# Tokens transposed without their norm, layer 3's norm factor applied at the banks, six context k-tiles first, and another ending, in a four-layer backbone on one core

## The chip, the cores and the metric

The kernel runs on one core of a Trainium2 chip. What counts is the device time of one execution in microseconds (us). The kernel before took 2101.03 us, the median of three timed runs (2100.48 to 2101.74). One further execution was recorded by the hardware profiler; it took 2097.56 us.

## The reference, cut to what matters

A latent stream of 256 tokens and a context stream of 256 tokens, both 2048 wide and in float32, pass through four layers: Fourier mixing, mLSTM, attention, and Fourier mixing again. Every layer normalises the tokens, scales and shifts them by factors made from a conditioning vector, mixes them, and adds the gated result to the residual. The last layer works on the latent stream alone, and a normalisation ends the whole.

```python
for i in range(DEPTH):
    shift, scale, gate = jnp.split(sc @ ada_w[i] + ada_b[i], 3, axis=-1)
    hx = _rmsnorm(x, norm_g[i]) * (1.0 + scale[:, None]) + shift[:, None]
    ...   # the same for the context, with its own shift, scale and gate
    y_x = branch(hx)      # Fourier: (fourier_mix(hx) * silu(hx @ w_gate)) @ w_out
    x = x + gate[:, None] * y_x
    ...
return _rmsnorm(x, final_g)
```

`_rmsnorm(x, g)` is `x * rsqrt(mean(x*x) + eps) * g`. The factor rsqrt(...), called rstd below, is one number for each token. "Stream 0" in the kernel is the context (columns 0 to 255 of a k-tile), "stream 1" the latent (columns 256 to 511).

## The kernel before

**Layout.** Activations lie transposed: 16 k-tiles, each 128 features by 512 token columns. A product in full precision is made of three matmuls in a faster 32-bit format: every operand is split into a high part (`h`, `wh`) and a low part (`l`, `wl`), and h·wh, h·wl and l·wh are summed in a PSUM bank (line 309). Weights stream in as 512 KB tiles for two k-tiles each (`make_w`, line 264); ScalarE makes `wh` (267), VectorE `wl` (268). Three such pairs are held (`WHL`).

**gemm (line 274).** In orientation A the weights are stationary and four banks of 128 output features by the token columns are filled; in orientation B the tokens are stationary and each bank holds 128 tokens by 512 output features. Eight weight tiles are walked through. For the last `tail` of them the loop goes bank by bank, so that one bank ends after the other and its `done` reads it while the next one is filled. With `begin`, used at the head of layers 1 and 2, the first four k-tiles are done for stream 0 alone, then for stream 1; `begin(kt)` is called after each k-tile of stream 0, and `Norm.begin` (429) uses it at k-tiles 0 and 2 for the two halves of stream 1's rstd: the column sums and their root (`rstd_cols`, 376), then the row that holds rstd for each token, spread over all partitions (`rstd_rows`, 392). `modulate` (401) makes h and l of one k-tile from the residual, the row, and the layer's factor and shift.

**Order.** Only TensorE's order is written out by hand; the instructions of the other engines are ordered by the framework's scheduler under their dependences. DMA starts lie on SyncE's queue, those of the last output partly on ScalarE's. Background work (`bg`, the conditioning products of later layers on VectorE, line 228) and filler work on TensorE (`fill`, `mixes`) are drawn from queues at hand-set rates, some steps for each piece of a gemm.

**Layer 0's start (lines 586 to 730).** The conditioning vector is spread over all partitions (`cb`, eight calls of `spread`, 239: VectorE builds diagonals, TensorE transposes them, VectorE copies the bank out). Four 1 MB tiles of tokens land; their squares are summed; r0 (rstd as a column) is made. `begin(k2, ...)` then runs for k2 = 0 to 7. It makes the scale and the shift of two k-tiles from eight 512 KB tiles of the conditioning weights (`ada_pe`, 189: the matmuls of line 198, four landings for the scale, then four for the shift), with pieces of layer 0's first gemm or of the Fourier mixing between them. For k2 = 0 the pieces are `turn(j)` (636): the tokens are multiplied by r0 (640, 642), transposed (646), and copied to `xT` (648). `modulated(k2)` (651) applies scale and shift on ScalarE (657) and splits into h and l (372, 373). The landing places are six buffers of their own and four of the `araw` pool; from k2 = 3 they are the four and up to three unused pairs of `l` tiles (`land_l`, 180).

**Layer 2's end and layer 3's head (lines 1270 to 1310).** `out_proj` (445) adds the gated product to the residual bank by bank (467) and sums squares (473, 474). Layer 3's scale and shift are finished. Then come the transposes of the residual to token-major `xtk` (1287, 1288), rstd as column and row, and `modulate` for each k-tile ahead of the gate product `gated(0)` (its `done` is line 1304).

**The ending (lines 1357 to 1394).** For every group of 512 output features and both banks of 128 tokens, `done` forms t = bank·gate and t = x + t (1376, 1377), sums its squares (1378), and apart from that makes t2 = bank·(gate·final_g) (1385) and x = x·final_g + t2 (1386, 1387). In the last group the sum gives rstd (1381, 1382, 1389), which multiplies the 2048 columns on VectorE (1152 of them, 1391) and ScalarE (896, 1392), and two DMAs carry them out.

Of the kernel before, what the change touches and what calls it, by code (L numbers as in the profile page):

```python
# [28 lines left out]
BR1O, BR2 = 0.5, 0.25  # L29
# [20 lines left out]
def _build(tc, nc, top, A, out):  # L50
# [23 lines left out]
    adab = cp.tile([P, 4, 3, 2, KT], F32, name="adab")  # L74
# [89 lines left out]
    def ada_finish(l, s, kts, src, nv):  # L164

        v0 = 2 - nv
        dst = ada[:, l, s, v0:2, kts]
        V.tensor_tensor(dst, src, adab[:, l, s, v0:2, kts], ALU.add)
        if s == SC:
            V.tensor_tensor(dst, dst, ng[:, l, v0:2, kts], ALU.mult)  # L170
# [9 lines left out]
    def land_l(kt):  # L180

        def get(src):
            raws = [hlp.tile([P, 512], F32, tag=f"l{k}", name=f"lraw{k}") for k in (kt, kt + 1)]
            for i in range(2):
                Q.dma_start(raws[i], src[:, i, :])
            return raws
        return get
# [51 lines left out]
    def spread(dst, col):  # L239

        d = ap_.tile([P, 2, 512], F32, tag="araw", name="adiag", bufs=ARAW)[:, 0, :]
# [34 lines left out]
    def gemm(hl, orient, t0, t1, done, first=False, used=None, halves=False, begin=None, tail=2):  # L276
# [46 lines left out]
        for k2 in range(2 if begin else 0, 8 - tail):  # L323
# [39 lines left out]

    def hl_pair(kt):
        h = hlp.tile([P, 512], F32R, tag=f"h{kt}", name=f"h{kt}")
        l = hlp.tile([P, 512], F32R, tag=f"l{kt}", name=f"l{kt}")
        return h, l
# [24 lines left out]
    def rstd_rows(pp, r, nt):  # L392

        ps = bank()
        for i in range(nt):
            d = pp.tile([P, 256], F32, tag="mu", name="rdiag", bufs=2)[:, :128]
            V.tensor_scalar(d, ones, r[:, i:i + 1], None, ALU.mult)
# [14 lines left out]
    class Norm:  # L412
# [16 lines left out]
        def begin(self, kt):  # L429
            if kt in (0, 2):  # L430
# [14 lines left out]
    def out_proj(pp, px, l, hl, old, new_dram, c0, rates, tag="xf", bufs=5, gate=None, norm=None, t0=None):  # L445
# [6 lines left out]
        for g in range(4):  # L452
# [5 lines left out]
            def done(b, ps, stream=None):  # L458
# [6 lines left out]
                for s in streams:  # L465
                    a = 256 * s - c0
                    V.scalar_tensor_tensor(rn[:, b, a:a + 256], ps[:, 256 * s - o:256 * s - o + 256],  # L467
                                           ada[:, l, GA, s, kt:kt + 1], ro[:, b, a:a + 256], ALU.mult, ALU.add)
                if kt == 0:
# [115 lines left out]
    with ExitStack() as st:  # L585
# [7 lines left out]
        for v in range(2):  # L593
            for j in range(4):
                o = cb[:, v, 512 * j:512 * j + 512]
                drain(spread(lambda ps, o=o: V.tensor_copy(o, ps), cvec[:, v, 4 * j:4 * j + 4]))
        ss = p0.tile([P, 4, 4], F32, name="ss")
        xt = []
        for j in range(4):
# [3 lines left out]
            for i in range(4):  # L603
# [3 lines left out]
                else:  # L607
                    junk = ap_.tile([P, 1024], F32, tag="junk", name="ajunk", bufs=1)[:, :512]
                    V.scalar_tensor_tensor(junk, x[:, i, :], 1.0, x[:, i, :], ALU.mult, ALU.mult,
                                           accum_out=ss[:, i, j:j + 1])  # L610
            if j == 2:

                S.activation(dummy, ss[:, 1, 2:3], AF.Sqrt)
            if j == 0:
                Q.dma_start(adab, A["adab"])
                Q.dma_start(ng, A["ng"])
        for l in range(4):

            V.tensor_scalar(adab[:, l, SC], adab[:, l, SC], 1.0, None, ALU.add)
# [3 lines left out]
        V.reciprocal(r0, r0)  # L623

# [9 lines left out]
        xT = []  # L634

        def turn(j):

            for t in range(4):
                if t % 2:
                    S.activation(xt[j][:, t, :], xt[j][:, t, :], AF.Copy, scale=r0[:, t:t + 1])  # L640
                else:
                    V.tensor_scalar(xt[j][:, t, :], xt[j][:, t, :], r0[:, t:t + 1], None, ALU.mult)
            for i in range(4):
                ps = bank()
                for t in range(4):
                    T.transpose(ps[:, 128 * t:128 * t + 128], xt[j][:, t, 128 * i:128 * i + 128], ident)
                x = hlp.tile([P, 512], F32, tag=f"h{4 * j + i}", name=f"xT{4 * j + i}")
                (S.copy if i % 2 else V.tensor_copy)(x, ps)
                xT.append(x)

        def modulated(k2):

            for kt in (2 * k2, 2 * k2 + 1):
                u = p0.tile([P, 512], F32, tag="mu2", name="u", bufs=2)
                for s in range(2):
                    c = slice(256 * s, 256 * s + 256)
                    S.activation(u[:, c], xT[kt][:, c], AF.Identity, scale=ada[:, 0, SC, s, kt:kt + 1],
                                 bias=ada[:, 0, SH, s, kt:kt + 1])
                hl[kt] = split_into(kt, u)

        araws, mixes = land(ap_, "araw", ARAW), Weave()

        def begin(k2, places):


            make_w()
            place = [places]
            for n, _ in enumerate(chain(*(ada_pe(0, s, k2, cpad, place) for s in (SC, SH)))):
                if k2 == 0:
                    if n % 2:  # L670
                        turn(n // 2)
                elif n in (1, 2, 5, 6):
                    next(first)
                else:
                    mixes.give(MIX0)
            modulated(k2)
# [9 lines left out]
        with ExitStack() as st2:  # L686
            pf = pool(st2, "l0f", reuse_waits="tile")

            def mixed(j):
                eo = pf.tile([P, 2, 2, 512], F32, tag="eo", name="eo", bufs=1)  # L690
                V.tensor_tensor(eo[:, 0], xt[j][:, 0::2, :], xt[j][:, 1::2, :], ALU.add)
                V.tensor_tensor(eo[:, 1], xt[j][:, 0::2, :], xt[j][:, 1::2, :], ALU.subtract)
# [4 lines left out]
            for k2 in range(3, 8):  # L697
                spare = [land_l(kt) for kt in (10, 12, 14) if kt > 2 * k2]
# [39 lines left out]
    bg.add("l3", ada_chain([(3, s, j, 1) for s in (SC, SH) for j in range(4)]))  # L738
# [11 lines left out]
    with ExitStack() as st:  # L750
# [10 lines left out]
        def gates():  # L761
# [7 lines left out]
            for k4 in range(4):  # L769
                for ip in range(2):  # L770
                    for q in range(4):
                        kt = 4 * k4 + q
                        T.matmul(pq[32 * q:32 * q + 32, :], gw[:, 0, 32 * kt:32 * kt + 32], hl[kt][ip].bitcast(F32),  # L773
# [237 lines left out]
        def load_y(kt):  # L1011

            if kt < 12:
                h, l = hl_pair(kt)
                Q.dma_start(l.bitcast(F32), ytd[kt])
                S.copy(h, l.bitcast(F32))
                V.tensor_tensor(l, l.bitcast(F32), h.bitcast(F32), ALU.subtract)
# [252 lines left out]
    with ExitStack() as st:  # L1270
        pr = pool(st, "r2", reuse_waits="tile")
        bg.finish("ga2")
        with ExitStack() as st2:
            pn = pool(st2, "r2n", reuse_waits="tile")
            rn, acc = out_proj(pn, pr, 2, hl, lambda g: resid[1][:, 4 * NT * g:4 * NT * (g + 1)].rearrange(
                "p (a b) -> p a b", a=4)[:, :, 256:512], None, 256, [(0.5, 0.12)] * 3 + [(0, 0)], bufs=6, t0=0)
            bg.finish("l3")
# [13 lines left out]
            turns = turn_x()  # L1291
            wait = lambda: next(turns, None)
            wait()
            rc = rstd_cols(pr, acc, (0, 1), "rc2", wait)
            rrow = rstd_rows(pn, rc, 2)
            drain(turns)
            hl = Lazy(lambda kt, rn=rn, rrow=rrow, pn=pn: modulate(3, kt, rn[kt // 4][:, kt % 4, :], rrow, pn, 1, None))
            sgs, mixed3, gated3 = [], set(), set()

            def gated(g):  # L1300
                def done(b, ps):
                    if b == 0:
                        sgs.append(pr.tile([P, 4, 256], F32, tag="xf", name="sg", bufs=6))
                    S.activation(sgs[g][:, b, :], ps, AF.Silu)
# [3 lines left out]
                return gemm(hl, "A", 256, 512, done, first=g == 0)  # L1308

            first = ahead(gated(0))  # L1310
# [51 lines left out]
        rf = p4.tile([P, 2], F32, name="rf")  # L1362
        for g in range(4):
            cols = slice(512 * g, 512 * g + 512)
            gf = []

            def done(b, ps):
                if b == 0:
                    if g == 0:
                        bg.finish("row3")  # L1370
                    w = p4.tile([P, 512], F32, tag="gf", name="gf", bufs=1)
                    V.tensor_tensor(w, gate3[:, cols], fg[:, cols], ALU.mult)
                    gf.append(w)
                x = xtk[:, b, cols]
                t = p4.tile([P, 512], F32, tag="x1", name="t4", bufs=3)
# [128 lines left out]
```

## Time and profile before

| | |
|---|---|
| median of three timed runs | 2101.03 us |
| the profiled execution | 2097.56 us |
| its span in the trace | 2095.8 us |
| TensorE busy | 2056.8 us (98%) |
| VectorE busy | 1569.3 us (75%) |
| ScalarE busy | 844.9 us (40%) |
| mean DMA rate over the span | 216 GB/s |

In the profile PE is TensorE's matmuls, PEld its weight loads, DVE VectorE, ACT ScalarE, SP SyncE; L309 is line 309 of the kernel. A row of the timeline gives the start, the duration, the engine, the line, the operation, output and inputs, the shape and the number of instructions merged into the row; brackets give idle time before it and what ended it. The ends of matmuls are modelled, so the spacing of starts says more than a duration. A row of the waits gives who waited for whom, the total in us, how often, and the longest. A row of the stages (windows) gives length, the busy time of PE, PEld, DVE, ACT and POOL with the number of instructions, the granted TensorE clock as a share of full speed, the DMA engines' busy share, and GB/s.

### The profile page before, as it was taken

To read this page: it belongs to the slowest core of one execution; us is meant where nothing else is said; L and a number is where in the kernel's file an instruction comes from. 1 tells how busy PE (TensorE), PEld (TensorE's weight loads), DVE (VectorE), ACT (ScalarE), POOL (GpSimd) and SP (SyncE) were. 2 spreads that over 40 slices of the span, in tenths; PEclk is the share of its full clock that TensorE was granted. 3 is DMA by queue.
4 is the path that set the end of the run, shared out by engine and by line. 5 is a ranking of instruction groups with operands and counts; after the bars stand their busy time and mean duration, and the time that the engine had idled before them with its cause. 6 is when DMAs were issued, how large, how long until landed. Compare 5 with 4: busy or idle time off the path is not lost.

```text
span 2095.8 us, 30020 instructions
## 1 busy us (share of the span) xinstructions
PE 2056.8 (98%) x11405; PEld 1726.5 (82%) x11405; DVE 1569.3 (75%) x2921; ACT 844.9 (40%) x1414; POOL 17.5 (1%) x29
## 2 busy tenths in 40 slices
PE   7999999999999999999999999999999999999997
PEld 4678777798788888888888888888888888999986
DVE  6578888837787898799776788865657886557766
ACT  5442232226343324323432343224645555455443
POOL 0000000000000000000000000000000000000000
PEclk9999999999999999999999999999999999999999
DMA  9966878863565665577667678983343554554464
GB/s 394 347 241 204 293 249 302 322 219 98 167 195 171 221 233 179 172 255 250 207 240 282 221 238 300 339 316 102 100 143 129 165 181 138 181 191 154 164 186 151
DMA packets 127601, 452.60 MB, mean 216 GB/s; under 512 B 14400, under 2 KB 16976, under 8 KB 124640
## 3 DMA queue, kind: packets, MB, share of 16 engines
q1 hardware_dynamic: 126992, 448.71, 62.9%
q8 instruction: 89, 1.46, 0.3%
q10 hardware_dynamic: 464, 1.97, 0.3%
q14 instruction: 56, 0.46, 0.1%
HBM read 436.96 MB, written 13.67 MB: 215 GB/s over the span
## 4 chain that ended last, share of the span: by engine, by line
PE 94%; DVE 3%; ACT 1%; DMA 1%; issue 0%; SPq 0%; ACTq 0%; DVEq 0%
PE acc L309 83%; PE xb L198 2%; PE xb L904 2%; PE xb L518 1%; PE xb L1178 1%; PE xb L551 1%; PE xb L856 1%; PE xb L1163 1%; DVE wl L268 1%; PE xb L892 1%; PE xb L773 0%; PE xb L944 0%; PE xb L1149 0%; PE xb L1147 0%; PE xb L1146 0%
## 5 line engine op out<-in xcount | busy, mean ns | idle before, releaser
L268 DVE TENSOR_TENSOR wl<-wraw,wh 128x1024 fp32r<-128x1024 f32 x400 | 488.6, 1223 | 356.9 <-ACT wh L267 342.9
L267 ACT CAST wh<-wraw 128x1024 fp32r<-128x1024 f32 x400 | 419.6, 1050 | 700.9 <-PE acc L309 598.4
L309 PE MATMUL acc<-h,wh 128*128 128x512 f32 (+1 forms) x1936 | 680.5, 351 | 6.3 <-ACT h L407 3.0
L309 PE MATMUL acc<-l,wh 128*128 128x512 f32 (+1 forms) x1936 | 670.8, 346 | 1.2 <-DVE l L408 0.8
L309 PE MATMUL acc<-h,wl 128*128 128x512 f32 (+1 forms) x1936 | 669.8, 346 | 0.1
L309 PEld LDWEIGHTS acc<-h,wh 128*128 128x128 f32 x1936 | 367.1, 190 | 63.6 <-issue 11.3
L309 PEld LDWEIGHTS acc<-l,wh 128*128 128x128 f32 x1936 | 366.8, 189 | 49.3 <-DVE l L373 2.2
L309 PE MATMUL acc<-wh,h 128*128 128x512 f32 x1024 | 405.8, 396 | 1.0 <-ACT h L407 1.0
L309 PEld LDWEIGHTS acc<-h,wl 128*128 128x128 f32 x1936 | 367.3, 190 | 42.3 <-DVE wl L268 0.6
L309 PE MATMUL acc<-wh,l 128*128 128x512 f32 x1024 | 400.1, 391 | 0.0
L309 PE MATMUL acc<-wl,h 128*128 128x512 f32 x1024 | 399.5, 390 | 0.0
L228 DVE SCALAR_TENSOR_TENSOR araw<-araw,cb 128x1024 f32<-128x1024 f32 x288 | 349.3, 1220 | 8.6 <-DMA araw<-in_ada_t_dram 7.5
L309 PEld LDWEIGHTS acc<-wh,l 128*128 128x128 f32 x1024 | 192.2, 188 | 41.6 <-DVE l L408 0.4
L309 PEld LDWEIGHTS acc<-wh,h 128*128 128x128 f32 x1024 | 192.4, 188 | 40.4 <-issue 3.6
L309 PEld LDWEIGHTS acc<-wl,h 128*128 128x128 f32 x1024 | 192.5, 188 | 35.7 <-issue 0.2
L228 DVE SCALAR_TENSOR_TENSOR ajunk<-araw,cb 128x1024 f32<-128x1024 f32 x160 | 196.1, 1226 | 0.0
L198 PE MATMUL xb<-araw,cpad 128*32 128x256 f32 x696 | 49.0, 396 | 5.6 <-ACT wh L267 3.6
L473 ACT ACTIVATE sq<-rn 128x256 f32<-128x256 f32 (+1 forms) x48 | 24.7, 515 | 55.6 <-DVE rn L467 53.8
L467 DVE SCALAR_TENSOR_TENSOR rn<-acc,ada,rold 128x256 f32<-128x256 f32 x80 | 36.0, 479 | 6.8 <-PE acc L309 6.6
L198 PEld LDWEIGHTS xb<-araw,cpad 128*32 128x32 f32 x696 | 19.1, 110 | 26.2 <-DMA araw<-in_ada_p_dram 6.9
L474 DVE TENSOR_TENSOR sqacc<-sqacc,sq 128x256 f32<-128x256 f32 (+1 forms) x48 | 26.1, 544 | 4.3 <-ACT sq L473 3.7
L372 ACT CAST h<-F 128x512 fp32r<-128x512 f32 (+1 forms) x32 | 15.9, 513 | 30.5 <-PE acc L309 28.4
(274 smaller groups left out, 1695.7 us busy)
## 6 DMA issues: line engine op xcount, KB each, us to landing
araw<-in_ada_t_dram SPq DMA_DIRECT2D x288, 512.0 KB, 5.1
wraw<-in_w1in_dram SPq DMA_DIRECT2D x128, 512.0 KB, 4.4
araw<-in_ada_p_dram SPq DMA_DIRECT2D x87, 512.0 KB, 7.2
wraw<-in_w2in_dram SPq DMA_DIRECT2D x80, 512.0 KB, 3.5
wraw<-in_w0g_dram SPq DMA_DIRECT2D x32, 512.0 KB, 6.4
wraw<-in_w0o_dram SPq DMA_DIRECT2D x32, 512.0 KB, 5.9
wraw<-in_w1o_dram SPq DMA_DIRECT2D x32, 512.0 KB, 6.8
wraw<-in_w2o_dram SPq DMA_DIRECT2D x32, 512.0 KB, 3.7
```

What stands on the lines that cost most here:

```text
L198: T.matmul(ps[32 * q:32 * q + 32, :256], cpad[:, 4 * kq + q, :], rv[q // 2][:, 256 * (q % 2):256 * (q % 2) + 256], start=kq == 0, stop=kq ...
L228: V.scalar_tensor_tensor(o, rv, 1.0, cb[:, v + 2 - nv, part], ALU.mult, ALU.mult, accum_out=am[:, v, i, hf:hf + 1])
L267: S.copy(wh, raw)
L268: pace.append(V.tensor_tensor(wl, raw, wh.bitcast(F32), ALU.subtract).ins)
L309: T.matmul(o, lhsT, rhs, start=start, stop=stop)
L467: V.scalar_tensor_tensor(rn[:, b, a:a + 256], ps[:, 256 * s - o:256 * s - o + 256], ada[:, l, GA, s, kt:kt + 1], ro[:, b, a:a + 256], ALU. ...
L473: S.activation(sq[:, c], rn[:, b, c], AF.Square)
L474: V.tensor_tensor(acc[0][:, c], acc[0][:, c], sq[:, c], ALU.add)
L518: T.matmul(ps[:, o:o + 128], eo[:, e, s, 128 * d:128 * d + 128], cm, start=True, stop=True)
L551: T.matmul(ps[:, o:o + w], M[:, par, i, :], mv(i), start=i == 0, stop=i == 1)
L856: T.matmul(sp[:, :ns], q[:, hh, dg], k[:, 2 + hh, :ns], start=ip == 0, stop=ip == 2)
L904: T.matmul(po[:, :256], w[:, 128 * k:128 * k + 128], v[:, k, 256 * hh:256 * hh + 256], start=k + ip == 0, stop=k == nb - 1 and ip == 2)
```

## The change

- **Start.** The tokens are transposed as they land, without r0; r0 is spread to a row tile (`rows`, in the `l` tile of k-tiles 14 and 15), and `modulated` multiplies `xT` by it on VectorE ahead of scale and shift. `cb` is spread inside `begin(0)`, copied by ScalarE. `begin(0)` takes its weight tile after the scale's landings. The Fourier mixing applies r0 itself, with one more step of its generator. `adab` is gone: the biases land in `ada`.
- **Low parts in pairs.** Tiles `l` are allocated for two k-tiles together; a spare landing place is one DMA of 512 KB, and there are two instead of three.
- **Heads of layers 1 and 2.** Six k-tiles of stream 0 come first; the two halves of stream 1's rstd are called at k-tiles 1 and 3; weight tiles are taken at even k-tiles.
- **Layer 3.** `out_proj` of layer 2 writes, for each k-tile, h and l of the residual times layer 3's scale. The shift lies in two more columns of the same tiles, so that the gate product has 258 columns. rstd multiplies the bank, and the product of weights and shift is the bias of the Silu. The gate product starts before the transposes and rstd, which go between its pieces. The wait for layer 3's scale is for one of four parts at a time.
- **Ending.** x takes the residual and then the gain; gate·gain and its product are gone. The last group's tail is three weight tiles, and each half of the tokens goes out in four parts.
- The background rate in layer 2's `out_proj` is 0.05 for 0.12.

```diff
@@ gemm
-                for kt in range(4):
+                for kt in range(6):
                     hl.half(kt, s)
-                    if s == 0 and kt in (0, 1):
+                    if s == 0 and kt % 2 == 0:
                         ws.append(next_w())
-        for k2 in range(2 if begin else 0, 8 - tail):
+        for k2 in range(3 if begin else 0, 8 - tail):
@@ Norm.begin
-            if kt in (0, 2):
+            if kt in (1, 3):
                 self.piece(1, kt // 2)
@@ start, as each token tile lands
+            for i in range(4):
+                ps = bank()
+                for t in range(4):
+                    T.transpose(ps[:, 128 * t:128 * t + 128], x[:, t, 128 * i:128 * i + 128], ident)
+                o = hlp.tile([P, 512], F32, tag=f"h{4 * j + i}", name=f"xT{4 * j + i}")
+                (S.copy if i % 2 else V.tensor_copy)(o, ps)
...
+        rows = hlp.tile([P, 2, 512], F32, tag="l7", name="rows")[:, 0, :]
+        drain(spread(lambda ps: S.copy(rows, ps), r0, p0))
@@ modulated
+                V.tensor_tensor(u, xT[kt], rows, ALU.mult)
...
-                    S.activation(u[:, c], xT[kt][:, c], AF.Identity, scale=ada[:, 0, SC, s, kt:kt + 1],
+                    act = S.activation(u[:, c], u[:, c], AF.Identity, scale=ada[:, 0, SC, s, kt:kt + 1],
@@ begin
-                    if n % 2:
-                        turn(n // 2)
+                    next(spreads, None)
+                    next(spreads, None)
...
+                if k2 == 0 and n == 3:
+                    make_w()
@@ layer 0, spare places
-                spare = [land_l(kt) for kt in (10, 12, 14) if kt > 2 * k2]
+                spare = [land_l(kt) for kt in (10, 12) if kt > 2 * k2]
@@ layer 2's out_proj, layer 3's head
+            def scaled(kt, x):
+                if kt % 4 == 0:
+                    bg.finish(f"l3{kt // 4}")
+                h, lo = hT[kt]
+                S.activation(h[:, 256:512], x, AF.Copy, scale=ada[:, 3, SC, 1, kt:kt + 1])
+                V.scalar_tensor_tensor(lo[:, 256:512], x, ada[:, 3, SC, 1, kt:kt + 1], h[:, 256:512].bitcast(F32),
+                                       ALU.mult, ALU.subtract)
...
+            for kt in range(KT):
+                for i in range(2):
+                    (S.copy if i else V.tensor_copy)(hT[kt][i][:, 512:514],
+                                                     shift[:, i, kt:kt + 1].bitcast(F32).to_broadcast([P, 2]))
...
-                    S.activation(sgs[g][:, b, :], ps, AF.Silu)
+                    S.copy(c, ps[:, 256:257])
+                    V.tensor_tensor(sg, ps[:, 0:256], rrow, ALU.mult)
+                    S.activation(sg, sg, AF.Silu, bias=c)
...
-                return gemm(hl, "A", 256, 512, done, first=g == 0)
+                return gemm(hT, "A", 256, 514, done, first=g == 0)
...
+            def wait(n=1):
+                for _ in range(n):
+                    next(first)
+                    next(turns, None)
+            wait(4)
+            rc = rstd_cols(pr, acc, (0, 1), "rc2", lambda: wait(2))
...
@@ ending
+            V.tensor_tensor(t, ps, gate3[:, cols], ALU.mult)
+            V.tensor_tensor(x, x, t, ALU.add)
+            S.activation(ps, x, AF.Square, accum_out=acc)
...
+            V.tensor_tensor(t, xtk[:, b, 1536:], fg[:, 1536:], ALU.mult)
+            r, x, o = rf[:, b:b + 1], xtk[:, b, :], out[0, 128 * b:128 * b + 128, :]
+            V.tensor_reduce(r, ss4[:, b, :], AX.X, ALU.add)
+            S.activation(r, r, AF.Sqrt, bias=eps1, scale=1.0 / D)
+            V.reciprocal(r, r)
+            for c in (slice(0, 576), slice(576, 1152)):
+                V.tensor_scalar(x[:, c], x[:, c], r, None, ALU.mult)
+                Q.dma_start(o[:, c], x[:, c])
+            for c, src in ((slice(1152, 1536), x[:, 1152:1536]), (slice(1536, 2048), t)):
+                S.activation(x[:, c], src, AF.Copy, scale=r)
+                S.dma_start(o[:, c], x[:, c])
...
-            run(gemm(hl, "B", 256, 512, done, first=g == 0), 0, 0.25)
+            run(gemm(hl, "B", 256, 512, done, first=g == 0, tail=3 if g == 3 else 2), 0, 0.25)
```

More of the change, by code (lines that the diff above doesn't have):

```diff
@@ L1290, in turn_x @@
                             yield 1
[L1291 to L1297, printed above, removed]
+            bg.finish("l3s")
+            shift = p3.tile([P, 2, KT], F32R, name="shift")
+            S.copy(shift[:, 0, :], ada[:, 3, SH, 1, :])
+            V.tensor_tensor(shift[:, 1, :], ada[:, 3, SH, 1, :], shift[:, 0, :].bitcast(F32), ALU.subtract)
+            for kt in range(KT):
+                for i in range(2):
+                    (S.copy if i else V.tensor_copy)(hT[kt][i][:, 512:514],
+                                                     shift[:, i, kt:kt + 1].bitcast(F32).to_broadcast([P, 2]))
             sgs, mixed3, gated3 = [], set(), set()
```

162 lines of the change are left out of this document (84 added, 78 removed).

## The prediction

> **What bounds the kernel now.** First the page: TensorE is busy almost throughout.
>
> ```profile
> PE 2056.8 (98%) x11405; PEld 1726.5 (82%) x11405; DVE 1569.3 (75%) x2921; ACT 844.9 (40%) x1414; POOL 17.5 (1%) x29
> ```
>
> So a change gains either by less work for PE or by less of its idle time, which is 2095.8 - 2056.8 = 39 us in all. The next view was the waits of PE alone, asked for in stretches, to see where these 39 us lie. The four places that the change touches answer as follows (layer 0 from 40 to 136 us; the heads of layers 1, 2 and 3):
>
> ```profile
> PE acc L309 <- ACT h L372: 2.1, 3, 1.2
> PE xb L198 <- DMA araw<-in_ada_p_dram: 1.6, 3, 1.0
> ```
>
> ```profile
> PE acc L309 <- ACT h L407: 1.0, 1, 1.0
> PE xb L383 <- DVE sqacc L474: 0.9, 1, 0.9
> ```
>
> ```profile
> PE xb L383 <- DVE sqacc L474: 1.1, 1, 1.1
> PE acc L309 <- ACT h L407: 1.0, 1, 1.0
> ```
>
> ```profile
> PE acc L309 <- ACT h L407: 2.0, 2, 1.1
> PE acc L309 <- DVE l L408: 0.8, 1, 0.8
> PE xb L383 <- ACT sqlast L478: 0.5, 1, 0.5
> ```
>
> That is 3.7, 1.9, 2.1 and 3.3 us. The rest lies mostly at the two ends of the span. Hence the third view, the stages of the start, in pieces of 20 us:
>
> ```profile
> 0.00:20.00 20.00, 8.29 (x48) 5.38 (x48) 16.21 (x41) 9.39 (x22) 0.20 (x4) 0.88 0.90 357
> 20.00:40.00 20.00, 18.38 (x162) 13.05 (x162) 12.98 (x27) 14.53 (x27) 0.00 (x0) 0.86 1.03 417
> 40.00:60.00 20.00, 18.91 (x176) 11.30 (x175) 9.05 (x21) 9.11 (x17) 0.00 (x0) 1.00 1.03 411
> 60.00:80.00 20.00, 20.00 (x169) 14.06 (x170) 7.26 (x20) 8.08 (x17) 0.00 (x0) 1.00 1.00 376
> ```
>
> PE idles 11.7 + 1.6 = 13.3 us ahead of 40 us. The column before the last is the DMA engines' share: they are full until 60 us and nearly so until 80, while PE still has idle time until 60 and none from 60 to 80. The start is therefore bound by the bytes of the conditioning weights up to about 60 us, and by PE's own work after that.
>
> **The start.** The change moves 64 transposes and the spreading of the conditioning vector into time in which PE waits for landings. But the first 60 us carry the same bytes in nearly the same order, so PE only reaches the same landings sooner and waits there. After 60 us its work is the same: the multiplication by r0 goes to VectorE (16 k-tiles), which was busy 9.05 of 20 us there; the Fourier pieces come one step later. The edit that gives the change its first name is worth close to nothing. What can move are the 3.7 us of waits. Those for landings can go, because two Fourier pieces now fall between the last landings; one spare landing place less can bring one back (1.0). The wait for h (1.2, the longest) comes after the last conditioning product and has the same chain of ScalarE in front of it. If the scheduler leaves the new VectorE product of 512 columns in that chain, it adds 0.68, by its nearest like:
>
> ```profile
> 2071.23 0.68 DVE L1372 TENSOR_TENSOR gf<-gate,fg 128x512 f32<-128x512 f32 x1
> ```
>
> Behind that wait the clock falls:
>
> ```profile
> 128.00:132.00 4.00, 2.46 (x13) 1.71 (x12) 3.65 (x13) 3.98 (x10) 0.00 (x0) 0.92 0.99 376
> 132.00:136.00 4.00, 4.00 (x17) 3.20 (x17) 4.00 (x10) 2.31 (x3) 0.00 (x0) 0.65 0.49 177
> ```
>
> The column behind POOL is the granted clock: 4 x 0.08 + 4 x 0.35 = 1.7 us of full-speed time are lost. I take a gain of 1.0 for the start, between a loss of 1.5 (one wait of 1.0, and two thirds of 0.68) and a gain of 3.5 (all waits but the longest, 3.7 - 1.2 = 2.5, and 1.0 of the 1.7 of slow clock).
>
> Does the clock stay up while PE has more transposes and fewer products at the start? In the kernel before it does:
>
> ```profile
> 24.00:28.00 4.00, 2.65 (x17) 2.01 (x16) 2.54 (x7) 3.97 (x8) 0.00 (x0) 0.80 1.03 423
> 28.00:32.00 4.00, 4.00 (x52) 2.90 (x51) 1.55 (x3) 1.54 (x3) 0.00 (x0) 1.00 1.03 413
> 32.00:36.00 4.00, 4.00 (x46) 3.54 (x48) 3.07 (x6) 3.24 (x7) 0.00 (x0) 1.00 1.02 413
> ```
>
> ```profile
> 31.31 1.86 PE L646 MATMUL xb<-cst,xt 128*128 128x128 f32 x15
> ```
>
> The Trainium skill, in "TensorE: Matmul & The Clock Gate", Part 4, says that transposes do not count as activity for the clock gate; by that the first products behind the moved transposes would run at half speed for one window (its Part 1 gives 3.4 us), an estimate of 1.7 us more. The rows show a full clock through a stretch filled with transposes, so I charge nothing; and DMA is what sets the pace there.
>
> **The heads of layers 1 and 2.** At each, PE waits twice. First for the sum of squares: the column sums of stream 1 are called after k-tile 0, VectorE is still at work on:
>
> ```profile
> 485.90 1.22 DVE L268 TENSOR_TENSOR wl<-wraw,wh 128x1024 fp32r<-128x1024 f32 x1
> 487.04 0.42 DVE L474 TENSOR_TENSOR sqacc<-sqacc,sq 128x256 f32<-128x256 f32 x1
> 487.37 0.48 DVE L408 SCALAR_TENSOR_TENSOR l<-mu,ada,h 128x256 fp32r<-128x256 f32 x1
> ```
>
> Called one k-tile later, the sums find the squares ready. But then k-tile 1 is what PE wants, and its l (L408) is the last row here: if VectorE keeps this order, a wait for l of about 0.8 takes the place of 0.9 to 1.1. I count 0.4 gained at each head (0 to 1.0). Second, PE waits 1.0 for h behind the row's transposes; now k-tiles 4 and 5 of stream 0 lie behind them, 24 products at layer 1. Their spacing comes from the chain that ended last, in stretches of unbroken work (columns: start, length, count; first 512 columns wide, then 256):
>
> ```profile
> 906.00 68.06 PE acc L309 x300
> ...
> 1787.37 90.72 PE acc L309 x756
> ```
>
> That is 0.227 and 0.120 each, so 24 x 0.12 = 2.9 us of cover against 1.0: this wait goes, with a spacing or so (0.16) that modelled ends hide. Two heads give 2 x (1.16 + 0.4) = 3.1. Against it, k-tiles 4 and 5 of layer 1 run as halves: 24 x (2 x 0.120 - 0.227) = 0.3. Net 2.8, from 0.7 (both new waits for l, and VectorE late for two more halved k-tiles) to 4.3 (all waits of 4.0 with their hidden spacings, less 0.3).
>
> **Layer 3.** PE goes from the last product of layer 2 into the gate product without rstd, so the 3.3 us go, with five hidden spacings of 0.16: 4.1. What could replace them are the copies of the shift: the first product needs them, and they come behind the last bank in program order. They depend on background work that is done long before:
>
> ```profile
> L228 DVE SCALAR_TENSOR_TENSOR araw<-araw,cb x11: 1208/1218/1228, 1653.5 to 1731.3; 128x1024 f32<-128x1024 f32 x11
> ```
>
> Its last start is 1731.3, before layer 2's output product starts (1787.37 above). So the background rate of 0.05 changes nothing, no wait for the scale's parts is added, and the copies can be made early. That the scheduler lifts such work over earlier lines is seen in the ending, where the product of line 1372, quoted above at 2071.23, stands in the program behind the last of the gemm's weight splits, and runs before that gemm is through (its last bank is read at 2085.03, below).
>
> If it does not, the first product waits for rn, h and copies, some 1.9 us (four steps like L408's 0.48). Costs: 768 products are 258 columns wide instead of 256, 768 x 0.120 x 2/256 = 0.7. Each of 16 banks is released by a copy and a VectorE product (like L474, 0.42) instead of one ScalarE read; between a bank's end and its next use lie 18 products, 2.2 us, which cover it; 0.3 for misses (0 to 1.5). In layer 2's output product each bank adds 0.48 on VectorE inside 1.44 us per bank, where it now has 0.48 + 0.42 and a share of the weight splits; 0.1 (0 to 1.0). Net 4.1 - 0.7 - 0.3 - 0.1 = 3.0, from 0.5 to 3.4.
>
> **The ending.** From the last bank on:
>
> ```profile
> 2085.03 0.69 DVE L1376 TENSOR_TENSOR t<-acc,gate 128x512 f32<-128x512 f32 x1
> ...
> 2088.36 0.69 DVE L1386 TENSOR_TENSOR xtk<-xtk,fg 128x512 f32<-128x512 f32 x1
> 2089.08 0.69 DVE L1387 TENSOR_TENSOR xtk<-xtk,t 128x512 f32<-128x512 f32 x1
> 2089.69 0.16 DVE L1389 RECIPROCAL rf<-rf 128x1 f32<-128x1 f32 x1
> 2089.88 0.82 DVE L1391 TENSOR_SCALAR xtk<-xtk,rf 128x1152 f32<-128x1152 f32 x1
> ```
>
> ```profile
> 2087.44 0.62 ACT L1378 ACTIVATE t<-t 128x512 f32<-128x512 f32 x1
> 2087.57 0.37 ACTq L1394 DMA_DIRECT2D out_dram<-xtk  x1
> 2087.96 0.19 ACT L1378 ACTIVATION_READ_ACCUMULATOR t<-t 128x1 f32 x1
> 2088.48 0.29 ACT L1382 ACTIVATE rf<-rf,eps 128x1 f32<-128x1 f32 x1 [0.33 <-DVE rf L1381]
> ```
>
> ```profile
> 2092.00:2094.00 2.00, 0.00 (x0) 0.00 (x0) 0.00 (x0) 0.00 (x0) 0.00 (x0) 0.50 1.01 398
> 2094.00:2096.00 2.00, 0.00 (x0) 0.00 (x0) 0.00 (x0) 0.00 (x0) 0.00 (x0) 0.50 0.09 34
> ```
>
> The reciprocal stands 4.66 us after the bank's first read, because the other bank's work (two engines) lies between. With a tail of three tiles the other bank ends 18 products x 0.227 = 4.1 us earlier instead of 2.7, and has less to do. Left is the plain chain: 0.7 + 0.7 + 0.62 + 0.2 + reduce 0.2 + root 0.3 + 0.05 for handovers = 2.8. So the scaling starts 2.0 us sooner. The output's 1 MB then needs 2.6 us at 398 GB/s whatever its pieces are; with first pieces of half the length it begins about 0.3 sooner. The three-tile tail needs its third tile after 12 x 0.227 = 2.7 us; split in two steps (wl takes 1.22, wh about as long), it is just in time; 0.1. Net 2.2, from 1.0 to 3.0.
>
> **Sum.** 1.0 + 2.8 + 3.0 + 2.2 = 9.0: the profiled 2097.56 would be 2088.6. The timed median lies 3.47 above the profiled run; kept as it is, 2101.03 - 9.0 = 2092.0. About 0.2% (4.2 us) is what a measurement of this kernel can tell from no change.
>
> **Rivals.**
> - *New waits at the heads.* VectorE keeps its order at layers 1 and 2, or falls behind with the halved k-tiles; the l of k-tile 1 is waited for instead of the sums, and the shift's copies sit late at layer 3. For it: the three rows of VectorE above follow without a pause. Then 1.0 + 0.7 + 3.0 - 1.9 + 2.2 = 5.0: 2096.0. Still faster.
> - *Given back.* All four terms near their lower ends: -1.5 + 0.7 + 0.5 + 2.2 = 1.9: 2099.1, no change to be told. For it: four queues are reordered at once. Against: the ending's gain hangs on none of the others.
> - *Slower: starved landings in layer 0*. With two spare places instead of three, and pairs that are freed together, the eight groups of landings of k2 = 4 to 7 each come late by the longest wait seen, 1.0, and each of the four rounds pays the slow clock seen once, 1.7: 8 + 6.8 = 14.8 lost against 8.0 gained elsewhere: 2107.8. It decides from the point at which PE meets a wait over about 1 us in every round. Against: PE had no idle time at all from 60 to 80 us, and the round with no spare place had only 1.6 us in waits for landings. The skill's Part 1, with its window of 3.4 us, has the same slow clock behind idle time; rows here show it behind one of four such waits.
> - *The early transposes are worth what PE idles before 40 us*, some 5 of 13 us, if the bytes are not what bounds the start: 2087. Against: the DMA share of 1.03.
>
> **How the numbers follow.** Forecast 0.62; new waits at the heads 0.15; early transposes worth more 0.05; given back 0.12; slower 0.06. Faster is the first three, 0.82; within 0.2% 0.12; slower 0.06. The low end takes the high ends in part and the last rival: 2087.0. The high end takes the lower ends of all terms: 2099.5.
>
> **What would show it.** Right: the first gemm of layer 0 starts sooner, but PE reaches 60 us no further ahead; the waits for L474 and L407 at the heads of layers 1 and 2 shrink from 4.0 to about 1; no PE wait of over 0.3 between layers 2 and 3; reciprocal to scaling within 2.9 us of the last bank. Wrong: waits for landings between 80 and 125 us over 3 us; a wait for l at k-tile 1 of over 0.8; a first gate product that waits for a copy; matmuls of 258 columns spaced wider than 0.122.

## The result, and the profile after

The changed kernel takes 2114.78 us (median of 6 runs, 2111.93 to 2115.44), the kernel before 2100.85 in the same session: a ratio of 1.0063, 95% interval 1.0050 to 1.0076. It is 14 us slower, where 9 us faster was forecast; the range ended at 2099.5. The profiled execution of after takes 2111.93 us, with a span of 2110.1. Of all the executions reported below one, of the last kernel, took 2551.77 us at a granted clock of 0.751 where the others have 0.99 or more; that kernel's ratio is taken from its other four.

First the busy times, from the page of after:

```profile
span 2110.1 us, 30101 instructions
PE 2080.0 (99%) x11433; PEld 1724.7 (82%) x11433; DVE 1563.9 (74%) x2933; ACT 853.1 (40%) x1455; POOL 18.1 (1%) x29
```

PE was busy for 2056.8 us of 2095.8; now it is for 2080.0 of 2110.1. Its idle time went from 39.0 to 30.1 us, close to the 9 us forecast, and its *busy* time grew by 23 us with 28 matmuls more. So the waits aren't where the time was lost. At the heads of the layers they nearly went, while those for landings in layer 0 grew from 1.6 us to 3.7; these are PE's waits in after from 40 to 136 us, at the head of layer 1, at that of layer 2, and from 1925 us to the end (columns: waiter, releaser, us in total, times, longest; from 1865 to 1925 us, the head of layer 3, the view has no row at all):

```profile
PE xb L196 <- DMA araw<-in_ada_p_dram: 3.7, 9, 0.6
PE acc L307 <- ACT h L376: 0.9, 1, 0.9
PE acc L307 <- DVE l L377: 0.5, 1, 0.5
...
PE acc L307 <- DVE l L415: 0.3, 1, 0.3
...
PE acc L307 <- DVE l L415: 0.5, 2, 0.3
...
PE acc L307 <- DVE sg L1349: 0.4, 2, 0.2
```

The heads of layers 1 and 2 wait for 0.8 us instead of 4.0, that of layer 3 for nothing instead of 3.3. Next the chain that ended last, at the place that the prediction took its spacing from (start, length, count):

```profile
719.19 69.62 PE acc L307 x300
914.70 69.62 PE acc L307 x300
1110.20 69.62 PE acc L307 x300
```

The same 300 products, unbroken in both kernels, took 68.06 us before: 0.2269 us each, and now 0.2321. The stretches of 100 us say the same without any modelled end: from 1000 to 1100 us PE is busy throughout, at the full granted clock (the column 1.00), in the kernel before and then in after:

```profile
1000.00:1100.00 100.00, 100.00 (x490) 83.89 (x489) 71.56 (x141) 39.04 (x76) 1.66 (x3) 1.00 0.67 223
```

```profile
1000.00:1100.00 100.00, 100.00 (x479) 82.58 (x478) 72.51 (x149) 41.05 (x82) 3.51 (x4) 1.00 0.62 207
```

490 matmuls fit into 100 us before, 479 after; of the products of 512 columns with h, l and the weights, 382 start there before and 373 after. Such a count speaks only where the same work falls into the stretch: from 500 to 600 us it rises, from 477 to 498, because the change puts more products of 256 columns there. What got longer are all those products of 512 columns, in every layer and whichever operand moves; three groups (busy, mean ns) in the kernel before and then in after:

```profile
L309 PE MATMUL acc<-wh,h 128*128 128x512 f32 x1024 | 405.8, 396 | 1.0 <-ACT h L407 1.0
L309 PE MATMUL acc<-wh,l 128*128 128x512 f32 x1024 | 400.1, 391 | 0.0
L309 PE MATMUL acc<-wl,h 128*128 128x512 f32 x1024 | 399.5, 390 | 0.0
```

```profile
L307 PE MATMUL acc<-wh,h 128*128 128x512 f32 x1024 | 410.0, 400 | 0.0
L307 PE MATMUL acc<-wh,l 128*128 128x512 f32 x1024 | 403.9, 394 | 0.5 <-DVE l L415 0.5
L307 PE MATMUL acc<-wl,h 128*128 128x512 f32 x1024 | 403.5, 394 | 0.0
```

From one start to the next, those of 512 columns that follow one another directly take 227.7 ns before and 232.2 after (6,052 of them in after, 27 us); those of 256 columns 119.9 and 118.5 (1,653, 2.4 us back). Together 25 us, against the 23 us that PE is busy longer.

Three explanations were to be told apart. **A**: the addresses. The shift's two columns made the tiles of h and l 514 columns wide, so that they begin 2,080 bytes apart in a partition (514 floats are 2,056 bytes, and the framework places tiles at multiples of 32; an l of an odd k-tile lies 2,056 behind its neighbour) and no longer 2,048, the length of a row of 512 floats; before, every row that a gemm reads lay a whole number of rows from every other. **B**: any other address than before. **C**: contention with what else the change adds. Against C stands the trace. 504 products of 512 columns in after had neither VectorE nor ScalarE nor GpSimd at work from their start to the next one's, at a mean spacing of 231.6 ns; in the kernel before, 475 such had 227.2. Nor is it the DMA engines: 927 products of after had no packet in flight beside them, at 232.1 ns; before, 889 such had 227.6.

### The profile page after: what moved, and what is told of

The parts are those of the page before. It is cut to its first block, busy times and chain, and to the rows that moved or that the text cites. A ratio compares the mean times of both kernels' runs of the same rounds, so it can differ in the third digit from the quotient of the medians.

```text
span 2110.1 us, 30101 instructions
## 1 busy us (share of the span) xinstructions
PE 2080.0 (99%) x11433; PEld 1724.7 (82%) x11433; DVE 1563.9 (74%) x2933; ACT 853.1 (40%) x1455; POOL 18.1 (1%) x29
## 4 chain that ended last, share of the span: by engine, by line
PE 93%; DVE 3%; DMA 3%; ACT 1%; issue 1%; SPq 0%; DVEq 0%
PE acc L307 82%; DMA araw<-in_ada_p_dram 2%; PE xb L196 2%; PE xb L934 2%; PE xb L527 1%; PE xb L560 1%; PE xb L1209 1%; PE xb L886 1%; DVE wl L266 1%; PE xb L922 0%; PE xb L1194 0%; PE xb L803 0%; PE xb L974 0%; PE xb L1180 0%; PE xb L1147 0%
## 5 line engine op out<-in xcount | busy, mean ns | idle before, releaser
L307 PE MATMUL acc<-h,wh 128*128 128x512 f32 (+2 forms) x1944 | 685.3, 353 | 1.6 <-ACT h L376 0.9
L307 PE MATMUL acc<-l,wh 128*128 128x512 f32 (+2 forms) x1944 | 675.8, 348 | 0.9 <-DVE l L377 0.5
L307 PE MATMUL acc<-h,wl 128*128 128x512 f32 (+2 forms) x1944 | 674.1, 347 | 0.0
L482 ACT ACTIVATE sq<-rn 128x256 f32<-128x256 f32 (+1 forms) x48 | 24.5, 511 | 44.9 <-DVE rn L474 43.1
```

What stands on the lines that cost most here:

```text
L307: T.matmul(o, lhsT, rhs, start=start, stop=stop)
L482: S.activation(sq[:, c], rn[:, b, c], AF.Square)
```

## The experiments

All ratios are against the kernel before, run on the same chip (medians 2099.3 to 2101.9 us).

**The tiles alone.** Two kernels separate the address from the work. In both the bias rows land in `ada`, which frees 1,536 bytes:

```
-    adab = cp.tile([P, 4, 3, 2, KT], F32, name="adab")
-        V.tensor_tensor(dst, src, adab[:, l, s, v0:2, kts], ALU.add)
+        V.tensor_tensor(dst, src, dst, ALU.add)
```

> The kernel before with one part of the change alone: the bias rows land in the tile of the factors, and the tile of 1,536 bytes a partition that held them goes. All tiles that follow in SBUF move down by 1,536 bytes, and they move together: the distance between any two operands of a matmul stays. Theory A (the matmuls of 512 columns are slower because the rows of their operands no longer lie a whole multiple of 2,048 bytes apart): no change, 2100.9 us within 2, spacing 226 to 227 ns. Rival B (it is the absolute address that counts): spacing above 229 ns and 2115 us or more. Rival C (the tiles don't matter; the other work that the change adds beside the matmuls slows them): no change.

Measured: 2099.64 us, ratio 0.9998 (0.9989 to 1.0007). The second widens the tiles and uses no more of them than before:

```
-        h = hlp.tile([P, 512], F32R, tag=f"h{kt}", name=f"h{kt}")
-        l = hlp.tile([P, 512], F32R, tag=f"l{kt}", name=f"l{kt}")
-        return h, l
+        h = hlp.tile([P, 514], F32R, tag=f"h{kt}", name=f"h{kt}")
+        l = hlp.tile([P, 514], F32R, tag=f"l{kt}", name=f"l{kt}")
+        return h[:, 0:512], l[:, 0:512]
```

> The same as the run with the bias rows folded in, and the tiles of h and l are 514 columns wide, of which 512 are used: no instruction is added, only addresses move (2,080 bytes from tile to tile in place of 2,048). Theory A: the spacing of 512 columns goes from 227.6 to about 232 ns, and with some 6,480 such matmuls at 4.4 ns the time is 2129 us (2118 to 2136). Rival B: as theory A, if any address does. Rival C: 2101 us within 2, spacing 227.6 ns.

Measured: 2120.78 us, ratio 1.0097 (1.0082 to 1.0113). Not one instruction is added, and 21 us are lost. The chain and the busy time of this kernel:

```profile
915.37 69.65 PE acc L308 x300
```

```profile
PE 2078.1 (98%) x11405; PEld 1722.0 (81%) x11405; DVE 1570.4 (74%) x2921; ACT 844.9 (40%) x1414; POOL 16.9 (1%) x29
```

C falls. The middle of the expectation was 8 us too high, in part because it left out that products of 256 columns get faster (118.2 ns against 119.9, 3.8 us over 2,315 of them).

**How far out of step.** An unused tile ahead of the weights' pool moves them against h and l:

```
+    gap = wp.tile([P, 8], F32, name="gap")      # 8 floats are 32 bytes; 16, 32, 64, 128 in the others
+    V.memset(gap, 0.0)
```

> The same as the run with the bias rows folded in, and 32 bytes that nothing reads lie between the tiles of h and l and those of the weights. Every h and l still lies a multiple of 2,048 bytes from every other, and every wh and wl likewise, but the two sets are 32 bytes out of step. Theory A in its first form (the stationary operand of the next matmul, loaded while one streams, must be in step with the moving one): slower, 2110 to 2130 us. Theory A in its second form (successive moving operands must be in step with one another, whatever the stationary one): no change, 2101 us within 2. Rival C: no change.

> The same with 64 bytes. If it were enough that an operand starts on a line of 64 bytes as the others do, no change: 2100 us within 2. With a period of 256 or 512 bytes: slower, 2115 to 2135 us, as with 32 bytes.

> As the runs with 32, 64, 256 and 512 bytes between the tiles of h and l and those of the weights, with 128 bytes. 32 and 64 bytes cost 28.8 and 11.6 us, 256 and 512 nothing. If 128 bytes are the period, no change: 2100 us within 2, spacing 227.6 ns. If it is 256, the operands are half a period out of step: slower, 2105 to 2130 us, spacing 229 ns or more.

> The same with 256 bytes. If 256 bytes are the period, no change: 2100 us within 2, spacing 227.6 ns. If it is 512, the operands are half a period out of step: slower, 2115 to 2135 us, spacing 230 ns or more.

> As the run with 32 bytes between the tiles of h and l and those of the weights, with 512 bytes there. The slices of 128 columns that a matmul loads as its stationary operand lie 0, 512, 1,024 and 1,536 bytes into a row already, and in the kernel before all four have a spacing of 227 ns. Theory A with a period of 512 bytes: no change, 2100 us within 2, spacing 227.6 ns. Theory A with a period of 2,048 bytes between whole rows: slower, 2110 us or more. Rival D (any gap shifts something else, the weights' own landings and splits among it, and that is what costs): slower, as with 32 bytes, near 2128 us.

| bytes | us | ratio (95%) | spacing, 512 columns, h and l moving / weights moving | 256 columns |
|---|---|---|---|---|
| 0 | 2099.64 | 0.9998 (0.9989 to 1.0007) | 227.6 / 227.8 ns | 119.9 ns |
| 32 | 2128.39 | 1.0131 (1.0115 to 1.0146) | 233.2 / 233.1 | 118.3 |
| 64 | 2111.38 | 1.0052 (1.0035 to 1.0070) | 233.3 / 229.5 | 115.6 |
| 128 | 2125.19 | 1.0120 (1.0101 to 1.0140) | 232.9 / 232.8 | 118.7 |
| 256 | 2100.23 | 1.0000 (0.9991 to 1.0009) | 227.6 / 227.8 | 119.9 |
| 512 | 2099.01 | 0.9998 (0.9989 to 1.0008) | 227.6 / 227.8 | 119.9 |

The chains of these kernels, with 32, 64, 128 and 256 bytes:

```profile
918.39 69.99 PE acc L310 x300
```

```profile
917.71 69.11 PE acc L310 x300
```

```profile
918.50 69.99 PE acc L310 x300
```

```profile
907.73 68.06 PE acc L310 x300
```

The period is 256 bytes: a gap of 256 or 512 costs nothing, one of 128 costs 25 us, and all the weights' splits and landings move with each of them, so rival D falls too. The second form of theory A falls with 32 bytes: there h and l agree with one another, wh and wl likewise, and it still costs 28.8 us. 64 bytes were expected to cost as much as 32 and cost less than half, for two reasons in the table: with the weights moving the spacing rises by 1.7 ns only, and products of 256 columns gain 4.3.

**Step or address?** In all the kernels so far that kept their time the tiles began 160 bytes past a multiple of 256 (so they never lay on lines of 64 bytes, as the expectation for 64 bytes had it). Two kernels move all operands together, by 32 and by 96 bytes (an unused tile at the end of the constants' pool):

> The kernel before with the bias rows folded in, and 32 bytes that nothing reads ahead of all tiles of h, l and the weights: every operand of the matmuls moves by 32 bytes, and all stay in step with one another. In all runs so far that kept 2100 us the tiles began 160 bytes past a multiple of 256, so it isn't known yet whether it is their common step that counts or this address. Theory A (the step between them): no change, 2100 us within 2, spacing 227.6 ns. Rival B (the address within 256 bytes): slower, 2110 us or more, spacing 229 ns or more.

Measured: 2099.71 us, ratio 1.0008 (0.9998 to 1.0017).

> The changed kernel with tiles in step (the run of 2091.6 us), with 96 bytes that nothing reads ahead of all tiles of h, l and the weights, which then begin at multiples of 256 bytes. Theory A (the step between them): the same as that run, 2091.6 us within 2, spacing 227.6 ns. Rival B (the address within 256 bytes): another time, slower by 10 us or more if 160 is the good one, or faster than 2088 us if multiples of 256 are better still.

Measured: 2092.79 us, ratio 0.9964 (0.9951 to 0.9977). Their chains:

```profile
905.60 68.06 PE acc L310 x300
```

```profile
905.75 68.09 PE acc L310 x300
```

B falls: at 192 and at 0 bytes past a multiple of 256 the operands are as fast as at 160. It isn't where they lie but how they lie to one another.

**Which pair?** With the gap placed between h and l, h alone is out of step; l, wh and wl agree:

```
+            if k2 == 0:
+                gap = hlp.tile([P, 8], F32, name="gap")
+                V.memset(gap, 0.0)
             modulated(k2)
```

> The kernel before with the bias rows folded in, and 32 bytes that nothing reads between the tiles of h and those of l: l, wh and wl are in step with one another, and h alone is 32 bytes out of step with them. Theory A1 (what counts is the moving operand that streams against the stationary operand that is loaded meanwhile for the next matmul): with h and l moving, the spacing after h,wh and h,wl is near 233 ns and after l,wh 227; with the weights moving, it is near 233 after wh,h and wh,l and 227 after wl,h, during which l is loaded. Theory A2 (the matmul's own stationary operand): the same with h and l moving, but with the weights moving near 233 after wh,h and wl,h and 227 after wh,l. Theory A3 (one moving operand against the next): with the weights moving all are 227. By A1 and A2 the time is 2119 us (2112 to 2124), two thirds of the 28.8 us that 32 bytes between all pairs cost; by A3 less than 2112.

Measured: 2127.57 us, ratio 1.0130 (1.0113 to 1.0147). The chain of this kernel:

```profile
919.28 70.00 PE acc L308 x300
```

All three versions miss, in the time and in the pattern: the spacing is 233.8, 234.2 and 231.5 ns after h,wh, h,wl and l,wh, and 234.8, 232.9 and 231.4 after wh,h, wl,h and wh,l. By one version or another l,wh, wh,h, wl,h and wh,l should have been at 227; none is. So a product slows down even when it, its own stationary operand and the one loaded next are in step, if its neighbours in the queue are not. What in the chip links them stays open. The Trainium skill, in "TensorE: Matmul & The Clock Gate", Part 2, says that loading the next weights doesn't steal read bandwidth from the running matmul, since each has its own port. No run here shows the two apart; what the runs do show is that the spacing depends on how the two sets of operands lie to each other in SBUF, with 233 ns at 32 bytes and 227.6 at 256, which that rule alone would not give.

**The change, in step.** The two shift columns go ahead of the data, into columns that layer 2 has done with, and the tiles are 512 wide again. The low parts lie in single tiles again too, no longer in pairs; that the width alone costs the time was seen above, where the tiles were widened without being paired:

```
-    (S.copy if i else V.tensor_copy)(hT[kt][i][:, 512:514],
+    (S.copy if i else V.tensor_copy)(hT[kt][i][:, 254:256],
...
-                    S.copy(c, ps[:, 256:257])
-                    V.tensor_tensor(sg, ps[:, 0:256], rrow, ALU.mult)
+                    S.copy(c, ps[:, 0:1])
+                    V.tensor_tensor(sg, ps[:, 2:258], rrow, ALU.mult)
...
-                return gemm(hT, "A", 256, 514, done, first=g == 0)
+                return gemm(hT, "A", 254, 512, done, first=g == 0)
```

> The changed kernel with all its parts, but tiles of h and l of 512 columns: the two shift columns of layer 3 are written to columns 254 and 255, ahead of the data, once the matmuls of layer 2 have read these, and not to 512 and 513 behind it. l of two k-tiles lands as two transfers again. Theory A: the spacing of 512 columns is back at 227.6 ns, the gains of the forecast show, and the time is 2086 to 2092 us (2114.8 less 6,480 times 4.4 ns is 2086). Rival C: still 2110 to 2115 us, with a spacing of 232 ns.

Measured: 2091.58 us (2088.40 to 2093.42), ratio 0.9953 (0.9941 to 0.9966). It beats both kernels, and the forecast for the change was 2092.0. The page and the chain of this kernel:

```profile
PE 2055.5 (98%) x11433; PEld 1725.9 (83%) x11433; DVE 1562.7 (75%) x2933; ACT 853.2 (41%) x1455; POOL 16.6 (1%) x29
```

```profile
906.19 68.06 PE acc L308 x300
```

The same 11,433 matmuls take 24.5 us less of PE than in after.

**The start, undone.** The last kernel keeps all that and puts layer 0 back as it was, with three spare landing places.

> The changed kernel with tiles in step, as in the run of 2091.6 us, but with layer 0 as before: tokens transposed with their norm, the context spread at the start; the heads of layers 1 and 2, layer 3 and the ending stay changed. By the forecast's term the new start is worth 1.0 us, so this is 2092.6 us, within its bounds 2090 to 2095. By the profiles of the two kernels (layer 0's second gate group ends at 208.5 us in the kernel before and at 210.2 with the new start) the new start costs 1.7 us, so this is 2089.9 us. The difference of the two is about what 5 rounds can tell.

Measured: 2089.70 us, ratio 0.9949 (0.9935 to 0.9962). The median is that of the second reading, but the intervals of the two kernels overlap almost wholly; it can only be said that the new start gains nothing that 5 rounds can tell.

## Why the prediction was wrong

The step that failed is the one that stands in the prediction as "That is 0.227 and 0.120 each" and "After 60 us its work is the same": spacings read from the kernel before were carried over to the kernel after, as if a product's time were fixed by its columns and the clock. Its opening, that the change gains by less work for PE or by less of its idle time, left no place for the same work taking longer. All that the prediction charged for the two columns was 0.7 us, for the 768 products that are two wider. That every tile of h and l gets wider for them, and so every row moves, was read in the diff and given no cost at all. The term left out measures 23.2 us (2114.78 - 2091.58, in two sessions; 24.5 of PE's busy time in the two profiles), two and a half times the sum of the others. No rival held it either: all of them were about waits and landings. The nearest sign named, products of 258 columns spaced wider than 0.122 us, would not have caught it: in after they have 0.120.

The other steps can be read from the kernel in step. The table gives times between events of the instruction records (a stage ends with the start of its last product with wh), in profiles with the old and with the new form of each part:

| term | forecast (bounds) | old form, us | new form, us | gain |
|---|---|---|---|---|
| start: end of layer 0's second gate group | 1.0 (-1.5 to 3.5) | 196.7 to 199.0, six profiles | 197.7 and 199.1 | none that shows |
| head of layer 1: last group of layer 0 to first of layer 1 | 1.4 | 48.1 | 46.4 | 1.7 |
| head of layer 2, likewise | 1.4 | 47.3 | 45.8 | 1.6 |
| layer 3: end of layer 2 to end of the gate groups | 3.0 (0.5 to 3.4) | 118.4 (120.5 in one of five profiles) | 114.5 | 3.9 |
| ending: last product's start to the span's end | 2.2 (1.0 to 3.0) | 11.2 | 9.1 | 2.1 |

- **The start.** Right in its reason, that transposing early only reaches the same landings sooner; generous by 1.0. PE idles for 10.7 us of the first 20 and 2.0 of the next; in after, from 0 to 80 us:

```profile
0.00:20.00 20.00, 9.26 (x65) 8.49 (x66) 12.08 (x36) 12.61 (x30) 0.20 (x4) 1.00 0.90 358
20.00:40.00 20.00, 17.97 (x174) 10.22 (x178) 12.18 (x24) 10.89 (x20) 0.00 (x0) 0.91 1.03 417
40.00:60.00 20.00, 18.34 (x161) 11.38 (x154) 11.32 (x23) 10.92 (x20) 0.00 (x0) 1.00 1.03 415
60.00:80.00 20.00, 19.12 (x162) 12.71 (x161) 9.33 (x22) 8.18 (x15) 0.00 (x0) 1.00 0.98 372
```

  The DMA engines' share from 20 to 60 us is 1.03 as before, and PE is hardly further ahead at 60 us: it has begun the same 224 products of the conditioning weights, and 55 products of the first gemm where it was 51. That the waits for landings would go was wrong. From 40 to 136 us they come to 3.7, 4.5 and 5.1 us in the three profiles with the new start, against 1.6 to 3.1 in the six with the old one: the rival of starved landings in small, 2 to 3 us where it had 8. What varies from profile to profile is the wait for h near 130 us with the slow clock behind it: 0.9 us in after with the clock at 1.00, and in the kernel in step

```profile
PE acc L308 <- ACT h L371: 2.0, 1, 2.0
```

```profile
128.00:132.00 4.00, 2.57 (x5) 1.20 (x5) 4.00 (x7) 3.93 (x7) 0.00 (x0) 0.71 0.84 293
```

  This agrees with that one ending the stage at 199.1, and the kernel moved by 96 bytes, with a wait of 0.9 and the clock at 1.00, at 197.7. The rule of the Trainium skill that was weighed there ("TensorE: Matmul & The Clock Gate", Part 4: transposes don't count as activity for the clock) isn't what this trace shows. In after PE's first 64 matmuls are the moved transposes, and nothing runs on PE beside them: they start 0.213 us apart until 9.96 us, 0.109 us apart from 10.1 us on, and a full clock is on record from 10.02 us, 3.1 us after the first. (The row above has 1.00 for 0 to 20 us because time ahead of the first record counts as full.) So it was right to charge nothing, on a row that showed less than was said: of the 50 matmuls that start from 28 to 32 us before, 18 are transposes.

- **The heads.** 3.3 us against 2.8, and what was left are waits for l, 0.3 us in all at the one and 0.6 at the other, none longer than 0.3. They begin at k-tile 1, as the alternative order of VectorE had it, though shorter than its 0.8.
- **Layer 3.** 3.9 against 3.0, beyond the upper bound of 3.4. The 0.7 for wider products wasn't paid: in the kernel in step those of 258 columns have a spacing of 119.5 ns, those of 256 one of 119.9 (in after, out of step, 120.3 and 118.5). That the copies of the shift would not be waited for was right in both kernels, although in the kernel in step they can start only once layer 2 has read the columns. The banks of layer 3 cost waits of 0.4 in after, 0.4 in the kernel in step, against 0.3 allowed.
- **The ending.** 2.1 against 2.2. The rows of after from the last bank on; the reciprocal starts 2.73 us behind the first read (forecast 2.8, before 4.66):

```profile
2101.67 0.69 DVE L1425 TENSOR_TENSOR t<-acc,gate 128x512 f32<-128x512 f32 x1 [0.32 <-PE acc L307]
2102.40 0.69 DVE L1426 TENSOR_TENSOR xtk<-xtk,t 128x512 f32<-128x512 f32 x1
2103.12 0.69 DVE L1432 TENSOR_TENSOR t<-xtk,fg 128x512 f32<-128x512 f32 x1
2103.88 0.16 DVE L1434 TENSOR_REDUCE rf<-ss 128x1 f32<-128x4 f32 x1
2104.40 0.16 DVE L1436 RECIPROCAL rf<-rf 128x1 f32<-128x1 f32 x1 [0.36 <-ACT rf L1435]
```

So of the four terms of the sum, the heads and the ending came out near their size, layer 3 above its bound, and the start at nothing. That they add up to 9.3 us against 9.0, and that the kernel in step lands within 0.5 us of the forecast time, is in part luck: 0.9 too little at layer 3 makes up for 1.0 too much at the start. The time is wrong by a term that the sum didn't have. (Two smaller slips of the sum: the lower ends of all terms add up to a gain of 0.7, so the range should have ended at 2100.3 and not at 2099.5; and 4.66 less 2.8 is 1.9, not 2.0. Neither changes the outcome.) In after itself the gains are hidden below the loss: 23 us lost, 9 gained, 14 slower.

## What to carry to other kernels

When a diff changes the shape of a tile that TensorE reads, work out the byte addresses of all its operands, before and after, ahead of any wait: here 8 bytes more in a row cost each of some 6,500 products 4.5 ns, more than all the waits that they helped to remove. For products like these, of 512 columns, keep rows that are multiplied with one another a multiple of 256 bytes apart, and find room for odd columns inside the row, or in columns that are free by then. A spacing read from the kernel before holds for the kernel after only as long as the layout does; the first thing to check in a profile after is the matmuls' count in a stretch where PE is busy throughout with the same work in both kernels.

## What the runs showed of the hardware

- The start-to-start time of float32r products of 512 columns depends on how their operands lie to one another in SBUF modulo 256 bytes: 227.6 ns in step, 229.5 to 233.3 with the weights 32, 64 or 128 bytes off. Moving everything together by 32 or 96 bytes changes nothing.
- One operand of four out of step (h by 32 bytes) slows all kinds of product, those that don't use it too: 231.4 to 234.8 ns.
- Products of 256 columns go the other way: 119.9 ns in step, 118.3 at 32 bytes and 115.6 at 64. So for a kernel with narrow products only, being in step need not be the best; no run here tried one.
- Transposes alone raised the clock: in after, with nothing else on PE, their spacing fell from 0.213 to 0.109 us, 3.1 us behind the first of them.
- It isn't the other engines or the transfers: in after, the spacing is 231.6 ns where VectorE, ScalarE and GpSimd all rest, and 232.1 where no DMA packet is in flight.
